# A hybrid decoder block on one core: gate tiles stored by chunk group, gathered rows spread over the dense loop, an 8-rank look-up and reciprocal roots on GpSimd

## The chip, the cores and the metric

The kernel runs on one core of a Trainium2 chip. A core has TensorE (PE in the profile, its weight loads PEld), VectorE (DVE), ScalarE (ACT), GpSimd (POOL) and SyncE (SP, which here only issues DMAs), a scratch memory of 128 partitions (SBUF), accumulators (PSUM) and 16 DMA engines to the DRAM. The metric is the time of one execution on the device in microseconds, the median of the runs.

## The reference

One decoder layer for 1024 tokens of width 1024, in float32:

```python
h  = rmsnorm(x, mix_norm)
zc = h @ w_in                                   # q|k|v, z, beta, alpha of the DeltaNet; q, k, v of the attention
o  = concat(gated_deltanet(...), swa_sink_attention(...))
x  = x + o @ w_out
x  = x + peer(rmsnorm(x, ffn_norm), peer_wq, peer_keys, peer_u, peer_v)
x  = x + sigmoid(rmsnorm(x, ple_norm) @ ple_gate) * (p @ ple_proj)
out = rmsnorm(x, final_norm)

def peer(h, wq, sub_keys, u_tab, v_tab):        # 8 heads, 128 x 128 experts, 16 per head and token
    qry = (h @ wq).reshape(T, 8, 2, 128)
    sc = einsum("thpd,hpnd->thpn", qry, sub_keys)
    top_s, top_i = top_k(sc, 16)
    cand_s = top_s[:, :, 0, :, None] + top_s[:, :, 1, None, :]
    best_s, best_pos = top_k(cand_s, 16)        # of the 16 x 16 sums
    expert = take(cand_i, best_pos);  gates = softmax(best_s)
    act = gelu(einsum("td,thkd->thk", h, u_tab[expert]))
    return einsum("thk,thkd->td", gates * act, v_tab[expert])
```

u_tab and v_tab have 16,384 rows of 1024 each.

## The kernel before

The tokens stand in 8 blocks of 128. Every matrix product with float32r operands splits both sides into a high and a low part and makes three products (`mm3`).

The program has three stages. **Upstream** (`upstream`): `project` multiplies x by w_in for the two halves of the tokens; then, for groups of two blocks, `mixers` (DeltaNet and attention) and `retrieve` (w_out, the norm, the queries, the first top-k, `topk`). `topk` finds the 16 best sums of each head and looks up which pair of ranks each one was: in steps of `KC` ranks it compares positions with constants and sums over 16 candidates by a tree of additions on `get3`.

**The two ways of PEER.** For the blocks in `ABLK` (5, 6, 7) the rows of u and v that each token chose are gathered by indirect DMA on GpSimd's queue: 128 fetches of u rows per block, each followed by a reduction on VectorE into `dots` (line 839), and 128 of v rows, each followed by an addition into `acc` (line 847). For the blocks in `BBLK` (0 to 4, `NT` = 640 tokens) everything is multiplied instead: `topk` builds a gate matrix of 128 x 128 experts per token. Four tokens at a time, VectorE makes two one-hot tiles (`o1`, `o2`), ScalarE scales `o2` by the gates, TensorE multiplies them into `bk_gm`, and ScalarE writes the result into `stage` (expert chunk by token). Every `TB` = 32 tokens a stage goes to `gd` in DRAM.

**The dense loop** (`dense`) runs over 128 chunks of 128 experts, in 32 groups of `GC` = 4. At a group's start the gate tile `Gt` is loaded (one buffer). Per chunk, u and v are loaded (`ur`, `vr`) and split, `bk_u` = u h is made in two parts of 320 tokens (24 matmuls each), ScalarE applies the gelu (`ge`), VectorE multiplies by `Gt` and splits the result into `wh` and `wl`. After four chunks, ten tiles of the output (5 blocks x 2 halves) are multiplied: four stay in PSUM (`bk_yp`) over all groups, six (`bk_y`, two banks) are added to `xB` on VectorE in every group. The gathering is a generator; after each chunk it is moved on by 6 rows, so that 24 rows per group are issued in the program's text ahead of the output tiles. Rows of block 5 use the 4 buffers of pool `gp`, those of blocks 6 and 7 also the 4 of `gx`.

**The last stage** (`final`) does the gate product, the projection and the final norm, block by block.

`rsqrt` makes a reciprocal root on VectorE by an integer guess and three Newton steps: 12 instructions. It is used for the 8 norms ahead of each of four products and twice per block in the DeltaNet, 48 times.

A scheduler places the instructions: it follows the order of the text as priority and a timeline of its own, and it fixes each engine's order when the program is built. On the chip each engine then runs its list in order. Where a tile's buffer is taken again, a wait stands in the queue that writes it.

Of the kernel before, what the change touches and what calls it, by code (L numbers as in the profile page):

```python
# [18 lines left out]
P = 128  # L19
# [8 lines left out]
GROUPS = [[0, 1], [2, 3], [4, 5], [6, 7]]  # L28
ABLK = [5, 6, 7]
BBLK = [0, 1, 2, 3, 4]  # L30
NA = len(ABLK)
GC = 4
TB = 32
GBUF = 4
GXBUF = 4
# [27 lines left out]
def block_kernel(ctx: ExitStack, tc, I, out, dbg=None):  # L63
    nc = tc.nc
    V, S, G, PE = nc.vector, nc.scalar, nc.gpsimd, nc.tensor
    NB = NBLK - NA
    NT = NB * P

# [39 lines left out]
    iota = cp.tile([P, P], F32, name="iota")  # L108
    sel_b = cp.tile([P, 3, 16, 8], BF, name="sel_b")
    early = ExitStack()  # L110
# [5 lines left out]
    UI, SL, ones = (C[n] for n in ("ui", "sl", "ones"))  # L116
# [3 lines left out]
    def load_consts():  # L120
        nc.sync.dma_start(ident, I["consts"][:, 0:P])
        nc.sync.dma_start(cst, I["consts"][:, P:])
        nc.sync.dma_start(iota, I["consts"][:, 4 * P:5 * P])
        V.tensor_copy(sel_b.rearrange("p s a h -> p (s a) h"), bc(sel[:, 58:106], 2, 8))
        V.memset(negt, NEG)
# [13 lines left out]
    h2d = dr.tile([max(NA, 1), P, D], F32, name="h2d")  # L139
    h2Td = [dr.tile([P, DK, NT], F32, name=f"h2Td{i}") for i in range(2)]  # L140
    gd = dr.tile([NT // TB, P, NE, TB], F32, name="gd")

    eidx = cp.tile([P, max(NA, 1), P], I32, name="eidx")
    gate_a = cp.tile([P, max(NA, 1), P], F32, name="gate_a")

    def rsqrt(pool, dst, src, scale, n):
        v = pool.tile([P, n], F32, tag=f"rsv{n}", name="rs_v")
        i = pool.tile([P, n], I32, tag=f"rsi{n}", name="rs_i")
        t = pool.tile([P, n], F32, tag=f"rst{n}", name="rs_t")
        V.tensor_scalar(v, src, scale, EPS, op0=ALU.mult, op1=ALU.add)  # L150
        V.tensor_scalar(i, v.bitcast(I32), 1, None, op0=ALU.logical_shift_right)
        V.tensor_scalar(i, i, -1.0, 1597463007.0, op0=ALU.mult, op1=ALU.add)
        y = i.bitcast(F32)
        for it in range(3):
            tt(t, y, y, ALU.mult)
            stt(t, t, -0.5, v, ALU.mult, ALU.mult)
            stt(dst if it == 2 else y, t, 1.5, y, ALU.add, ALU.mult)
# [169 lines left out]
    def upstream():  # L327
        with early as em:
            dn = em.enter_context(tc.tile_pool(name="dn", bufs=1, reuse_waits="tile"))
            psum(em, dn=2, de=1, sw=1)  # L330
            with ExitStack() as es:
# [21 lines left out]
                project(1, (c1, wp, sm))  # L353
            with ExitStack() as es:
                lt = es.enter_context(tc.tile_pool(name="lt", bufs=1, side="right", reuse_waits="tile"))
                retrieve = retrieving(lt, es)
                for gi in range(len(GROUPS)):
                    if gi + 1 < len(GROUPS):
                        mixers(gi + 1)
                    retrieve(gi)  # L360
# [20 lines left out]
    def retrieving(lt, es):  # L381
# [14 lines left out]
        def retrieve(gi):  # L396
# [9 lines left out]
            for ti in range(4):  # L406
# [11 lines left out]
                for bi in range(nb):  # L418
                    tt(xts[bi][:, cs], pcs[bi], xts[bi][:, cs], ALU.add)
            h2 = hp.tile([P, 2, DK, N], F32R, tag="h2", name="h2")  # L420
            h2h, h2l = h2[:, 0], h2[:, 1]
            for bi, b in enumerate(grp):
# [4 lines left out]
                if b in ABLK:  # L427
                    nc.sync.dma_start(h2d[ABLK.index(b)], h)
                transpose_split("s3", h, h2h, h2l, bs_)
                if b in BBLK:  # L430
                    t0 = (b - BBLK[0]) * P
# [4 lines left out]
            for q4 in range(4):  # L436
# [12 lines left out]
                for bi in range(nb):  # L449
# [5 lines left out]
                    for i in range(4):  # L455
                        first_topk(lt, sc[:, i], tv[bi][:, 4 * q4 + i], tiu[bi][:, 4 * q4 + i])
            for bi, b in enumerate(grp):
                topk(lt, bg, b, tv[bi], tiu[bi])

        return retrieve  # L460
# [52 lines left out]
    def deltanet(dn, dn_state, b, qkv_d, zc_d, g, beta, eg, mTh, mTl, cols):  # L513
# [3 lines left out]
        qkv = dn.tile([P, 12, P], F32, tag="qkv", name="qkv", bufs=2)  # L517
# [68 lines left out]
        for l in range(1, 7):  # L586
# [20 lines left out]
            if l < 6:  # L607
# [4 lines left out]
                copy(X, px)  # L612
        kb = scaled("kb", 4, cf[:, 2])
# [39 lines left out]
    def swa(dn, state, b, zc_d, cos, sin, sink, mTh, mTl, cols):  # L653
# [72 lines left out]
        state["kv"] = (kz, vz)  # L726

# [10 lines left out]
    def topk(tk, bg, b, v, iu):  # L738
# [13 lines left out]
        for h in range(8):  # L752
# [5 lines left out]
            V.max_index(out=pu[:, h, 8:16], in_max=bs[:, h, 8:16], in_values=c)  # L758
        pos = tk.tile([P, 16, 8], BF, tag="pos", name="pos")
# [6 lines left out]
        KC = 4  # L766
# [6 lines left out]
        for k0 in range(0, 16, KC):  # L773
# [13 lines left out]
            summed(i2.rearrange("p (h k) -> p k h", h=8)[:, ks], t3)  # L787

        ga = gate_a[:, ABLK.index(b)] if b in ABLK else bg.tile([P, P], F32, tag="ga", name="ga")
# [6 lines left out]
        tt(gv, gv, bc(gs, 2, 16), ALU.mult)  # L796
        if b in ABLK:
            stt(eidx[:, ABLK.index(b)], i1, 128.0, i2, ALU.mult, ALU.add)
            return
        pt = bank("gm", [4, P])  # L800
        tr(pt[:, 0], i1)
        tr(pt[:, 1], i2)
        tr(pt[:, 2], ga)
        tT = bg.tile([P, 3, P], F32, tag="tT", name="tT")
        copy(tT, pt[:, 0:3])
        NTK = 4
        for tb in range(P // TB):
            stage = bg.tile([P, NE, TB], F32, tag="stage", name="stage", bufs=2)
            for t8 in range(TB // NTK):
                c0 = tb * TB + t8 * NTK  # L810
                o1 = bg.tile([P, NTK, P], F32, tag="o1", name="o1", bufs=2)
                o2 = bg.tile([P, NTK, P], F32, tag="o2", name="o2", bufs=2)
                tt(o1, bc(iota, 1, NTK), bc(tT[:, 0, c0:c0 + NTK], 2, P), ALU.is_equal)
                tt(o2, bc(iota, 1, NTK), bc(tT[:, 1, c0:c0 + NTK], 2, P), ALU.is_equal)
                for i in range(NTK):
                    copy(o2[:, i], o2[:, i], scale=tT[:, 2, c0 + i:c0 + i + 1])
                for q in range(NTK // 4):
                    pg = bank("gm", [4, P])
                    for i in range(4):
                        mm(pg[:, i], o2[:, 4 * q + i], o1[:, 4 * q + i])  # L820
                    t0 = t8 * NTK + 4 * q
                    copy(stage[:, :, t0:t0 + 4].rearrange("p e t -> p t e"), pg)
# [225 lines left out]
```

## Time and profile before

| | |
|---|---|
| time, median of 3 runs | 3178.52 us (3174.45 to 3181.41) |
| span of the profiled execution | 3163.2 us, first to last instruction; its own time was not listed apart |
| TensorE busy | 2984.4 us (94%) |
| VectorE busy | 2601.3 us (82%) |
| ScalarE busy | 1296.5 us (41%) |
| GpSimd busy | 1028.0 us (32%) |
| moved by DMA | 869.38 MB, 275 GB/s on average |

In the profile's rows, a group of instructions shows its line, engine, operation, what it writes and reads, its count, then the busy time and the mean duration in ns, then the idle time of its engine just before it and what ended that. A matmul counts as busy until its modelled end. `L73`, `L76`, `L70` and `L128` are the lines of small helpers (`tt`, `stt`, `copy`, `mm`), so the tile names tell the place. A wait row reads: who waited, for whom, the sum in us, how often, the longest.

### The profile page before, as it was taken

What the parts mean: (1) busy time and instruction counts of PE and PEld (TensorE: products, weight loads), DVE (VectorE), ACT (ScalarE), POOL (GpSimd) and SP (SyncE); (2) the same over time, 40 slices, a digit from 0 to 9 for tenths busy, and PEclk for the clock granted to TensorE, in tenths of its full rate; (3) what the DMA queues carried; (4) which work ended last, traced back from release to release, by engine and by line L of the source; (5) the groups of instructions that cost most, each with busy time, mean ns of one, the idle gap of its engine ahead of it and who ended that gap; (6) DMA issues with size and microseconds to landing.
All of it is one profiled execution on the core that took longest, in us unless ns stands there. A gap on an engine that the chain in (4) does not pass through costs nothing. (4 is left out here: it accounts for less than half of the span.)

```text
span 3163.2 us, 50802 instructions
## 1 busy us (share of the span) xinstructions
PE 2984.4 (94%) x18287; PEld 2704.4 (85%) x18287; DVE 2601.3 (82%) x6191; ACT 1296.5 (41%) x2761; POOL 1028.0 (32%) x804
## 2 busy tenths in 40 slices
PE   7989989999897889899999999999999999999998
PEld 5878989899897878778888887988899889898887
DVE  6668636999899899789888887988988878799876
ACT  5577534488887862123222222222222122222232
POOL 0000000000000014445455565555565645566600
PEclk9999999999999999999999999999999999999999
DMA  7569566667578678778889888998998888999932
GB/s 232 159 240 353 171 213 225 207 228 248 199 242 321 235 274 283 279 263 298 292 297 316 305 310 310 338 353 304 340 334 309 315 317 321 327 328 345 334 140 87
DMA packets 366188, 869.38 MB, mean 275 GB/s; under 512 B 29296, under 2 KB 153584, under 8 KB 363120
## 3 DMA queue, kind: packets, MB, share of 16 engines
q1 hardware_dynamic: 255344, 463.43, 43.1%
q0 software_dynamic: 110592, 402.70, 35.3%
q8 instruction: 144, 2.36, 0.3%
q14 instruction: 108, 0.88, 0.1%
HBM read 766.40 MB, written 99.61 MB: 274 GB/s over the span
## 5 line engine op out<-in xcount | busy, mean ns | idle before, releaser
L128 PE MATMUL bk_u<-hT,uh 128*128 128x320 f32 x4096 | 919.4, 311 | 16.1 <-ACT ge L904 16.1
L833 POOL DMA_INDIRECT rows<-in_u_dram,eidx x384 | 495.1, 1289 | 893.6 <-DVE tiu L732 469.1
L128 PEld LDWEIGHTS bk_u<-hT,uh 128*128 128x128 f32 x4096 | 698.2, 189 | 36.6 <-ACT ge L904 19.3
L833 POOL DMA_INDIRECT rows<-in_v_dram,eidx x384 | 523.5, 1363 | 401.9 <-DVE acc L76 283.5
L128 PE MATMUL bk_u<-hT,ul 128*128 128x320 f32 x2048 | 635.8, 311 | 0.2 <-DVE ul L73 0.2
L76 DVE SCALAR_TENSOR_TENSOR acc<-rows,dots,acc 128x1024 f32<-128x1024 f32 x384 | 492.0, 1281 | 44.5 <-DMA rows<-in_v_dram,eidx 41.3
L839 DVE CUSTOM_DVE_ANT_0 rows<-rows,h2n 128x1024 f32<-128x1024 f32 x384 | 461.8, 1221 | 37.3 <-DMA rows<-in_u_dram,eidx 31.5
L128 PEld LDWEIGHTS bk_u<-hT,ul 128*128 128x128 f32 x2048 | 387.5, 189 | 5.0 <-DVE ul L73 0.5
L904 ACT ACTIVATE ge<-bk_u 128x320 f32<-128x320 f32 x256 | 110.3, 432 | 642.1 <-PE bk_u L128 541.9
L128 PE MATMUL bk_y<-vh,wh 128*128 128x512 f32 x768 | 313.1, 408 | 40.2 <-DVE xB L73 38.2
L70 ACT ACTIVATE wh<-ge 128x320 fp32r<-128x320 f32 x256 | 119.0, 470 | 525.6 <-DVE ge L73 466.7
L128 PE MATMUL bk_y<-vl,wh 128*128 128x512 f32 x768 | 308.5, 402 | 0.0
L128 PE MATMUL bk_y<-vh,wl 128*128 128x512 f32 x768 | 304.3, 402 | 2.2 <-DVE wl L73 1.8
L128 PE MATMUL bk_gm<-o,o 128*128 128x128 f32 x1280 | 205.4, 292 | 29.6 <-ACT o L70 27.6
L70 ACT ACTIVATE o<-o,tT 128x128 f32<-128x128 f32 x640 | 202.4, 396 | 40.0 <-DVE o L73 34.7
L73 DVE TENSOR_TENSOR o<-iota,tT 128x512 f32<-128x512 f32 x320 | 205.4, 686 | 13.8 <-PE bk_gm L128 12.9
L128 PE MATMUL bk_yp<-vh,wh 128*128 128x512 f32 x512 | 202.3, 400 | 13.5 <-ACT wh L70 13.5
L128 PEld LDWEIGHTS bk_gm<-o,o 128*128 128x128 f32 x1280 | 182.2, 200 | 37.1 <-ACT o L70 33.9
L73 DVE TENSOR_TENSOR ge<-ge,Gt 128x320 f32<-128x320 f32 x256 | 123.7, 487 | 108.7 <-DMA Gt<-gd 95.2
L128 PEld LDWEIGHTS bk_y<-vh,wh 128*128 128x128 f32 x768 | 147.8, 192 | 76.2 <-DVE xB L73 43.2
L128 PE MATMUL bk_s<-h,whi 128*128 128x256 f32 x1024 | 206.8, 294 | 5.2 <-ACT h L70 1.5
L128 PE MATMUL bk_yp<-vl,wh 128*128 128x512 f32 x512 | 201.8, 398 | 0.0
(308 smaller groups left out, 6001.8 us busy)
## 6 DMA issues: line engine op xcount, KB each, us to landing
ur<-in_uT_dram SPq DMA_DIRECT2D x128, 512.0 KB
vr<-in_v_dram SPq DMA_DIRECT2D x128, 512.0 KB
gd<-stage SPq DMA_DIRECT2D x20, 2048.0 KB
Gt<-gd SPq DMA_DIRECT2D x32, 1280.0 KB
wlo<-wqc SPq DMA_DIRECT2D x128, 256.0 KB
whi<-wqc SPq DMA_DIRECT2D x128, 256.0 KB
whi<-woc SPq DMA_DIRECT2D x64, 256.0 KB
wlo<-woc SPq DMA_DIRECT2D x64, 256.0 KB
```

The source lines that it names most:

```text
L70: return S.activation(o, i, AF.Copy, **k)
L73: return V.tensor_tensor(o, a, b, op)
L76: return V.scalar_tensor_tensor(o, a, s, b, op0, op1, **k)
L128: PE.matmul(o, l, r, start=start, stop=stop)
L833: G.indirect_dma_start(out=r, out_offset=None, in_=tab, in_offset=bass.IndirectOffsetOnAxis(ap=eidx[:, a, s:s + 1], axis=0))
L839: V.tensor_tensor_reduce(out=u, in0=u, in1=h2n, op0=ALU.mult, op1=ALU.add, scale=1.0, scalar=0.0, accum_out=dots[:, s:s + 1])
L904: S.activation(ge, pa, AF.Gelu_apprx_tanh)
```

## The change

- **Gate tiles.** `gd` is laid out by chunk group, [32 groups, 128, 40, 4, 16], and `TB` is 16. A group's `Gt` is now one contiguous run of 10 KB in each partition; a store of a stage (1 MB, 40 of them) has 32 runs of 256 bytes in each partition. The stage is evicted with the token as the innermost index, in runs of 4.
- **Rows.** The generator is moved on after each chunk and after each output tile, 768 rows over 448 steps. Each row's VectorE instruction is given a dependency on the dense loop's VectorE instruction three steps back (`LAG` = 2), which only sets the order. All three blocks take even rows from `gp` (4 buffers, opened before the last groups of the upstream stage) and odd rows from `gx` (3).
- **Chunks.** The next chunk's u and v are loaded and split in the text ahead of the output tiles (`prepared`).
- **Look-up.** `KC` is 8 in place of 4.
- **Roots.** `rsqrt` becomes a multiply-add and a power of -0.5 on GpSimd.
- **Space.** `qkv` has one buffer in place of two, the gates of blocks 0 to 4 take a part of `cand`, `iota` is read from the constants' tile.

`HBLK` is empty, so the branches for it, and the calls of `tick` in the upstream stage (no job is set there), issue nothing.

```diff
-BBLK = [0, 1, 2, 3, 4]
+DBLK = [0, 1, 2, 3, 4]
 ABLK = [5, 6, 7]
+BBLK = HBLK + DBLK          # HBLK = []
 GC = 4
-TB = 32
+TB = 16
 GBUF = 4
-GXBUF = 4
+GXBUF = 3
+LAG = 2
...
-    gd = dr.tile([NT // TB, P, NE, TB], F32, name="gd")
+    gd = dr.tile([NE // GC, P, NT // TB, GC, TB], F32, name="gd")
...
     def rsqrt(pool, dst, src, scale, n):
-        v = pool.tile([P, n], F32, tag=f"rsv{n}", name="rs_v")
-        i = pool.tile([P, n], I32, tag=f"rsi{n}", name="rs_i")
-        t = pool.tile([P, n], F32, tag=f"rst{n}", name="rs_t")
-        V.tensor_scalar(v, src, scale, EPS, op0=ALU.mult, op1=ALU.add)
-        V.tensor_scalar(i, v.bitcast(I32), 1, None, op0=ALU.logical_shift_right)
-        V.tensor_scalar(i, i, -1.0, 1597463007.0, op0=ALU.mult, op1=ALU.add)
-        y = i.bitcast(F32)
-        for it in range(3):
-            tt(t, y, y, ALU.mult)
-            stt(t, t, -0.5, v, ALU.mult, ALU.mult)
-            stt(dst if it == 2 else y, t, 1.5, y, ALU.add, ALU.mult)
+        v = pool.tile([P, n], F32, tag=f"rsv{n}", name="rs_v", bufs=2)
+        G.tensor_scalar(v, src, scale, EPS, op0=ALU.mult, op1=ALU.add)
+        G.tensor_tensor(dst, v, mhalf[:, 0:n], ALU.pow)
...
-        KC = 4
+        KC = 8
...
+            for t0 in range(0, TB, 4):
...
-                    copy(stage[:, :, t0:t0 + 4].rearrange("p e t -> p t e"), pg)
-            nc.sync.dma_start(gd[(b - BBLK[0]) * (P // TB) + tb], stage)
+                copy(stage[:, :, t0:t0 + 4], pg.rearrange("p t e -> p e t"))
+                yield
+            nc.sync.dma_start(gd[:, :, BBLK.index(b) * (P // TB) + tb].rearrange("g p c t -> p g (c t)"),
+                              stage.rearrange("p (g c) t -> p g (c t)", c=GC))
...
+    def fetched(gp, tab, u, s):
+        r = (pools["gx"] if "gx" in pools and s % 2 else gp).tile([P, D], F32, tag="rows", name="rows")
...
+            held_back(stt(acc, v, w[:, s:s + 1], acc, ALU.mult, ALU.add))
...
+    def held_back(ins):
+        if len(anchors) > LAG:
+            tc.add_manual_dep(ins.ins, anchors[-1 - LAG].name, ...)
...
+            def step(ins):
+                anchors.append(ins.ins)
+                count[0] += 1
+                n = total * count[0] // steps - count[1]     # steps = NE + NE // GC * NB * 2
+                count[1] += n
+                advance(n)
...
-                nc.sync.dma_start(Gt.rearrange("p t g k -> p t (g k)"),
-                                  gd[:, :, cg * GC:(cg + 1) * GC, :].rearrange("t p g k -> p t (g k)"))
+                nc.sync.dma_start(Gt, gd[cg])
...
-                    want = total * (c + 1) // NE
-                    while done < want and next(job, "end") != "end":
-                        done += 1
+                    if c + 1 < NE:
+                        nxt = prepared(c + 1)
+                    step(last)
...
                         if not keep or cg == NE // GC - 1:
-                            tt(xB[:, bi, cs], py, xB[:, bi, cs], ALU.add)
+                            last = tt(xB[:, bi, cs], py, xB[:, bi, cs], ALU.add)
+                        step(last)
```

Three places show what the scheduler makes of it. The first is SP's queue while the gates of block 2 go out; `whi` and `wlo` are the weights that TensorE needs for the queries of the next group, `keysT` the keys. Before:

```order
L393 DMA wlo_12244<-wqc1_85 128x512
L439 DMA keysT_12202<-in_keysT_dram 128x512
L823 DMA gd_72<-stage_9550 128x4096
L392 DMA whi_12274<-wqc0_84 128x512
L393 DMA wlo_12275<-wqc1_85 128x512
L392 DMA whi_12278<-wqc0_84 128x512
L393 DMA wlo_12279<-wqc1_85 128x512
```

And after the change:

```order
L394 DMA wlo_11959<-wqc1_86 128x512
L849 DMA gd_73<-stage_9332 128x32x64
L441 DMA keysT_11917<-in_keysT_dram 128x512
L393 DMA whi_11989<-wqc0_85 128x512
L849 DMA gd_73<-stage_9390 128x32x64
L394 DMA wlo_11990<-wqc1_86 128x512
L393 DMA whi_11993<-wqc0_85 128x512
L394 DMA wlo_11994<-wqc1_86 128x512
```

Stores stand twice as often among the weight loads, each of half the bytes, and each waits in this queue for its stage.

The second place is VectorE's list in the middle of the dense loop, where the output tiles of one group are added to `xB` while v rows are gathered. Before:

```order
L76 SCALAR_TENSOR_TENSOR acc_22999<-rows_23185,dots_20180,acc_22999 128x1024
L73 TENSOR_TENSOR xB_14844<-bk_y_23343,xB_14844 128x512
L76 SCALAR_TENSOR_TENSOR acc_22999<-rows_23188,dots_20180,acc_22999 128x1024
L76 SCALAR_TENSOR_TENSOR acc_22999<-rows_23191,dots_20180,acc_22999 128x1024
L73 TENSOR_TENSOR xB_14844<-bk_y_23357,xB_14844 128x512
L76 SCALAR_TENSOR_TENSOR acc_22999<-rows_23194,dots_20180,acc_22999 128x1024
L76 SCALAR_TENSOR_TENSOR acc_22999<-rows_23197,dots_20180,acc_22999 128x1024
L76 SCALAR_TENSOR_TENSOR acc_22999<-rows_23200,dots_20180,acc_22999 128x1024
L73 TENSOR_TENSOR xB_14844<-bk_y_23371,xB_14844 128x512
```

And after the change:

```order
L82 SCALAR_TENSOR_TENSOR acc_22342<-rows_23152,dots_19673,acc_22342 128x1024
L79 TENSOR_TENSOR xB_14178<-bk_y_23155,xB_14178 128x512
L82 SCALAR_TENSOR_TENSOR acc_22342<-rows_23169,dots_19673,acc_22342 128x1024
L82 SCALAR_TENSOR_TENSOR acc_22342<-rows_23172,dots_19673,acc_22342 128x1024
L79 TENSOR_TENSOR xB_14178<-bk_y_23175,xB_14178 128x512
L82 SCALAR_TENSOR_TENSOR acc_22342<-rows_23189,dots_19673,acc_22342 128x1024
L82 SCALAR_TENSOR_TENSOR acc_22342<-rows_23192,dots_19673,acc_22342 128x1024
L79 TENSOR_TENSOR xB_14178<-bk_y_23195,xB_14178 128x512
```

In the steady loop two or three rows stand between two additions to `xB` both before and after; the count no longer swings by three.

The third place is VectorE's list at the end of the dense loop and the start of the last stage, where `rs_t` and `rs_i` belong to a root, `h` to a norm, `wgl` to the gate weights. Before:

```order
L73 TENSOR_TENSOR rs_t_31092<-rs_i_31091 128x1
L76 SCALAR_TENSOR_TENSOR rs_t_31092<-rs_t_31092,rs_v_31090 128x1
L76 SCALAR_TENSOR_TENSOR rs_31089<-rs_t_31092,rs_i_31091 128x1
L73 TENSOR_TENSOR xB_14844<-bk_y_30899,xB_14844 128x512
L76 SCALAR_TENSOR_TENSOR h_31086<-xt_31082,rs_31089,ple_norm_30990 128x1024
L73 TENSOR_TENSOR xB_14844<-bk_y_30913,xB_14844 128x512
L73 TENSOR_TENSOR xB_14844<-bk_y_30927,xB_14844 128x512
L73 TENSOR_TENSOR xB_14844<-bk_y_30941,xB_14844 128x512
L73 TENSOR_TENSOR xB_14844<-bk_y_30955,xB_14844 128x512
```

And after the change:

```order
L79 TENSOR_TENSOR xB_14178<-bk_y_30260,xB_14178 128x512
L82 SCALAR_TENSOR_TENSOR acc_27716<-rows_30274,dots_25127,acc_27716 128x1024
L79 TENSOR_TENSOR xB_14178<-bk_y_30280,xB_14178 128x512
L82 SCALAR_TENSOR_TENSOR acc_27716<-rows_30277,dots_25127,acc_27716 128x1024
L82 SCALAR_TENSOR_TENSOR acc_27716<-rows_30294,dots_25127,acc_27716 128x1024
L82 SCALAR_TENSOR_TENSOR acc_27716<-rows_30297,dots_25127,acc_27716 128x1024
L82 SCALAR_TENSOR_TENSOR h_30326<-xt_30322,rs_30329,ple_norm_30320 128x1024
L79 TENSOR_TENSOR wgl0_30351<-raw_30352,wgh0_30350 128x1024
```

The last rows now stand behind the last output tile, and the first norm of the last stage behind them; the steps of the roots are gone from this list.

More of the change, by code (lines that the diff above doesn't have):

```diff
@@ L827, in gather_block, with gather_dots @@
+    def gather_dots(gp, u):
         h2n = gp.tile([P, D], F32, tag="hacc", name="h2n", bufs=1)
-        nc.sync.dma_start(h2n, h2d[a])
+        nc.sync.dma_start(h2n, h2d[u])
         dots = gp.tile([P, P], F32, tag="dots", name="dots", bufs=1)
-        def rows(tab, s):
-            r = (gx if a and s % 2 else gp).tile([P, D], F32, tag="rows", name="rows")
-            G.indirect_dma_start(out=r, out_offset=None, in_=tab,
-                                 in_offset=bass.IndirectOffsetOnAxis(ap=eidx[:, a, s:s + 1], axis=0))
-            return r
@@ L847, in gather_block, with half_job, gather_job, advance @@
         for s in range(P):
-            v = rows(I["v"], s)
-            stt(acc, v, w[:, s:s + 1], acc, ALU.mult, ALU.add)
+            v = fetched(gp, I["v"], u, s)
+            held_back(stt(acc, v, w[:, s:s + 1], acc, ALU.mult, ALU.add))
             yield
         nc.sync.dma_start(x1d[b], acc)
-    def gather_job(gp):
-        for a in range(NA):
-            yield from gather_block(gp, a)
+    def half_job():
+        for b in HBLK:
+            w = yield from gather_dots(pools["gp"], UBLK.index(b))
+            pt = bank("gm", [P])
+            tr(pt, w)
+            copy(slots[b][:, 2], pt)
+    anchors = []
+    def held_back(ins):
+        if len(anchors) > LAG:
+            tc.add_manual_dep(ins.ins, anchors[-1 - LAG].name,
+                              mybir.DependencyInfo(mybir.DependencyClass.NoSync, mybir.DependencyReason.DATA),
+                              reason="gather behind dense")
+    pools = {}
+    credit = [0.0]
+    def gather_job():
+        for b in ABLK:
+            yield from gather_block(pools["gp"], b)
+    def advance(n):
+        job = pools.get("job")
+        while job is not None and n > 0:
+            if next(job, "end") == "end":
+                pools["job"] = job = None
+            n -= 1
+    def drain():
+        advance(1 << 20)
+    def tick(us):
+        credit[0] += us * RATE
+        n = int(credit[0])
+        credit[0] -= n
+        advance(n)
     def dense(xB):
         with ExitStack() as es:
-            gp = es.enter_context(tc.tile_pool(name="gp", bufs=GBUF, reuse_waits="tile"))
             pp = es.enter_context(tc.tile_pool(name="pp", bufs=1, reuse_waits="tile"))
@@ L867, in dense @@
             held = {(bi, j): bank("yp") for bi in range(HELD) for j in range(2)}
-            hT = [pp.tile([P, DK, NT], F32R, name=f"hT{i}") for i in range(2)]
+            hT = [pp.tile([P, DK, NU], F32R, name=f"hT{i}") for i in range(2)]
             for i in range(2):
```

166 lines of the change are left out of this document (104 added, 62 removed).

## The prediction

> **What bounds the kernel now.** I read the busy shares by stage first, with borders at three events of the rows: the end of the gate building, the first product with a gate tile, and the last product of the dense loop.
>
> ```profile
> core 0: us, PE busy (x) PEld busy (x) DVE busy (x) ACT busy (x) POOL busy (x), PEclk, DMA share, GB/s
> 625.00:1150.00 525.00, 480.88 (x3837) 463.96 (x3835) 494.35 (x2037) 434.96 (x1083) 1.03 (x4) 0.97 0.70 243
> 1167.60:1923.40 755.80, 706.08 (x3772) 626.94 (x3771) 628.50 (x1149) 183.42 (x298) 383.08 (x293) 0.97 0.85 295
> 1923.40:3052.00 1128.60, 1115.09 (x6144) 1002.83 (x6144) 962.00 (x1327) 289.79 (x475) 631.38 (x473) 0.99 0.90 321
> 3052.00:3163.20 111.20, 97.22 (x448) 78.99 (x446) 79.46 (x239) 40.99 (x68) 0.00 (x0) 0.95 0.26 90
> 700.00:800.00 100.00, 99.13 (x845) 96.98 (x845) 98.73 (x420) 86.58 (x220) 0.00 (x0) 1.00 0.70 240
> ```
>
> From 625 to 1150 us the gates of blocks 0 to 4 are built, and VectorE is the fullest engine: 494 of 525 us. TensorE reads 481, but its 3837 matmuls go at 845 in 100 us where nothing holds it (last row), so it needs about 454 us. After 1167.6 us comes the dense loop, 32 groups of four chunks. Its pace, where it runs free, is in the chain that ended last:
>
> ```profile
> 2287.57 5.60 PE bk_y L128 x24
> ...
> 2343.72 5.60 PE bk_y L128 x24
> ...
> 2399.86 5.60 PE bk_y L128 x24
> ```
>
> One group is 56.15 us of pure TensorE. The loop has 32 x 56.15 = 1797 us of it, less about 7 us of a first chunk that is multiplied before 1167.6, so 1790; it takes 1884. So 94 us are lost there, nearly all in the first 756 us, where twelve groups (674 us less those 7) lose about 89. The waits say to what:
>
> ```profile
> DVE ge L73 <- DMA Gt<-gd: 95.2, 19, 8.6
> PE bk_y L128 <- DVE xB L73: 38.2, 15, 6.7
> DVE rows L839 <- DMA rows<-in_u_dram,eidx: 23.1, 26, 3.5
> DVE acc L76 <- DMA rows<-in_v_dram,eidx: 41.3, 36, 5.8
> 1904.76 0.08 DVE L839 DVE_READ_ACCUMULATOR2_ANT dots<- 128x1 f32 x1
> 1913.41 0.89 DVE L73 TENSOR_TENSOR ge<-ge,Gt 128x320 f32<-128x320 f32 x2 [8.58 <-DMA Gt<-gd]
> 1344.93 0.80 PE L128 MATMUL bk_y<-vh,wh 128*128 128x512 f32 x1 [6.65 <-DVE xB L73]
> ```
>
> VectorE stands 95 us for the gate tile (one buffer; its load starts when the last product of the group before has read it), 23 us for gathered u rows (up to 1500 us) and 41 us for v rows (1500 to 1850 us), in order, so the additions to xB behind it come late and TensorE finds no free bank. The clock column drops to 0.97 there.
>
> **The change, part by part.**
>
> *Gate tiles by group.* The load of a gate tile becomes 128 runs of 10 KB instead of 2560 of 512 bytes. The store becomes 163,840 runs of 256 bytes (40 x 128 x 32) instead of 2560 of 16 KB. Prices of a packet:
>
> ```profile
> q1 hardware_dynamic: 255344, 463.43, 43.1%
> q0 software_dynamic: 110592, 402.70, 35.3%
> q1 hardware_dynamic: 528, 0.26, 39.6%
> q1 hardware_dynamic: 47903, 126.85, 69.0%
> ```
>
> (The third row is a stretch of 2.2 us with one store to DRAM in 512-byte runs, the fourth 625 to 1150.) Shares are of 16 engines over the span of 3163.2 us: q0 161.5 ns for 3641 bytes, q1 85.4 ns for 1815 bytes, on average. The line through both is 9.8 ns + 0.0417 ns a byte: 31 ns at 512 bytes (the store itself: 0.396 x 16 x 2200 / 528 = 26 ns), 692 at 16 KB, and 20.4 ns at 256 bytes, an estimate. Loads: a group's tile takes 160 packets x 31 ns = 5.0 us per engine, interleaved with rows; after it 8 x 437 ns = 3.5 us, in 8 turns instead of 160. The 95 us of waits should go. Stores: 163,840 x 20.4 / 16 = 209 us of all engines against 2560 x 692 / 16 = 111. That is +98 us in 625 to 1150, where they were 0.70 x 525 = 368 us busy: 466.
>
> The Trainium skill, page "DMA: Bandwidth & Descriptors", section Specifications, asks for "≥512 B (below this, SDMA does read-modify-write)". No store of before is that short, so no run shows it; the rival below has its price.
>
> *Eviction.* ScalarE writes the stage with a stride; after the change it writes runs of four and reads PSUM with a stride.
>
> ```profile
> L70 ACT ACTIVATE stage<-bk_gm 128x512 f32<-128x512 f32 x160 | 170.4, 1091 | 28.0 <-PE bk_gm L128 27.0
> L70 ACT ACTIVATE X<-bk_dn 128x512 f32<-128x512 f32 x40 | 23.9, 599 | 38.6 <-PE bk_dn L131 38.6
> L76 DVE SCALAR_TENSOR_TENSOR rs_t<-rs_t,rs_v 128x1 f32<-128x1 f32 (+2 forms) x144 | 22.4, 158 | 2.5
> L73 DVE TENSOR_TENSOR get<-get 128x256 bf16<-128x256 bf16 x96 | 27.2, 284 | 0.5
> L73 DVE TENSOR_TENSOR get<-get 128x128 bf16<-128x128 bf16 x96 | 21.4, 222 | 0.4
> L73 DVE TENSOR_TENSOR get<-get 128x64 bf16<-128x64 bf16 x96 | 17.7, 184 | 0.4
> L73 DVE TENSOR_TENSOR get<-pos,sel_b 128x512 bf16<-128x512 bf16 x32 | 13.3, 417 | 0.2
> ```
>
> Between 0.60 (contiguous) and 1.09 us each, I take 0.72: 160 x 0.37 = 59 us less on an engine that has 90 us free in that stretch. Worth nothing by itself; it keeps ScalarE from being the next bound.
>
> *Powers on GpSimd.* 48 reciprocal roots of 12 VectorE steps at 0.157 us become two GpSimd steps each. VectorE is rid of 576 x 0.157 = 90 us, 60 of it ahead of the dense loop, the rest in the last stage.
>
> *Look-up of eight ranks.* 160 steps of 512 at 0.418 become 80 of 1024 at about 0.67 (0.5 ns an element by the rows of 128 and 256): 67 to 54 us. The trees, 96 x (0.284 + 0.222 + 0.184) = 66 us, become 48 x (0.41 + 0.284 + 0.222) = 44. Minus 35 us on VectorE.
>
> *Upstream sum.* About 60 of these 95 us lie in 625 to 1150 (nearly all of the look-up, half of the roots): VectorE 434, which at its present share of 0.94 makes a stretch of 461 (-64). TensorE allows 454 (-71). The DMA engines, at 0.94 (the fullest group of the dense loop shows that share), allow 466 / 0.94 = 496: **-29**. Late next is the weight load behind the stores on SP's queue. I take the smallest. Ends: -71, and +87 from the rival.
>
> *GpSimd's own price.*
>
> ```profile
> L679 POOL COPY vz<-qk 128x64 f32<-128x64 f32 x16 | 4.4, 306 | 419.6 <-DMA qk<-zcn 419.6
> L833 POOL DMA_INDIRECT rows<-in_u_dram,eidx x384 | 495.1, 1289 | 893.6 <-DVE tiu L732 469.1 <-DVE dots L839 294.6 <-issue 53.0
> POOL vz L675 <- PE bk_sw L128: 187.5, 5, 70.9
> 1846.99 6.39 DMA x1d<-acc
> 1853.39 3.85 DMA h2n<-h2d
> ```
>
> No power is in the trace. Two steps cost 0.6 us at the copy's price, 2.6 at the row fetch's, for 1.9 on VectorE: -1.3 to +0.7 a root, for 32 roots ahead of the loop -42 to +22 if all were exposed. I take 0: other blocks' work covers them, and a step of that few elements is nearest to the copy. If the cover fails, it is because they queue in order behind the clearing of vz, which waited up to 71 us for TensorE. The halved buffer of qkv costs a load of 768 KB per block behind the same cover: 0 to 8 x 3 us.
>
> *Rows spread and held.* No work is added; the order behind dense steps costs no semaphore, being on one engine. The first block gets seven buffers instead of four (later ones seven instead of eight), which removes most of the 64 us of row waits. What stays: the order puts 31 rows and the rest of the look-up into the first two groups, 126 us of VectorE at the rows' durations against 112 of TensorE, 14 us; and at five turns between u and v rows, and between blocks, VectorE waits for a store and a load (10 us, rows above) and catches up with 4.5 us of slack per group: 4 us each, 20. So 34 of 94 stay: **-60**, ends -85 and -15.
>
> *End.* Three row additions stand behind the last xB, 3 x 1.28 = 3.8 us, before the gate weights are split; the last root saves 1.3: **+2**.
>
> **Sum.** -29 - 60 + 2 = -87. The profiled execution spans 3163.2 us, 15 below the median of the runs shown, 3178.5, which I take as the frame around it: 3178.5 - 87 = 3091.5.
>
> **Rivals.**
>
> 1. *Short stores (slower).* If a 256-byte store costs no less than one of 512 (31 ns), the stores take 318 us, the DMA engines need 575, the stretch is 575 / 0.94 = 612, +87, and the time is 3178.5 + 87 - 60 + 2 = 3207. The sign turns at 28.4 ns a packet. For it: no shorter store is in the trace. Against it: the line through the two queues has a start of only 9.8 ns. If a short store is read and written back, two passes of 31 ns each, it is 637 us, a stretch of 951 and a time near 3547. The page named above says so; by its rule alone the change would be far slower.
> 2. *The dense loop keeps its loss.* VectorE works about 51 of 56 us in a group whatever feeds it; a row that lands late (the longest wait was 5.8 us) then stalls TensorE as the gate tile did. If 80 of the 94 us stay: 3178.5 - 29 - 14 + 2 = 3137. For it: one buffer fewer later on. Against: groups with eight buffers ran at 56 us.
> 3. *The engines allow more.* If the stores hide and VectorE sets the pace (-64), and only 19 us stay in the loop (-75): 3041.
> 4. *It does nothing*: the stores take back what the loop gains, by chance within 6 us of the old time.
>
> **How the numbers follow.** Forecast 0.59 (3050 to 3125 as its own range), rival 1 0.13, rival 2 0.14, rival 3 0.11, rival 4 0.03. Change within 0.2% (6 us, about what a measurement of this kernel can tell) is "same": 0.03; slower is rival 1, 0.13; faster the rest, 0.84. The range runs from 3035, just past rival 3, to 3165, which takes in rival 2 and a dearer GpSimd; rival 1 and a little at the bottom are left out.
>
> **What would show it.** Right: dense groups of 56 us from the first, hardly a wait of ge for Gt; the gate building shorter by some 30 us, with the DMA share there near 0.9; evictions near 0.7 us; VectorE's total down by about 125 us. Wrong: 256-byte packets well over 20 ns, or TensorE waiting for whi and wlo; GpSimd roots of several us, or stuck behind vz; waits of acc for rows in the later groups.

## The result, and the profile after

The changed kernel takes **3061.69 us** (median of 4 runs, 3061.11 to 3063.47), the kernel before 3178.68 (4 runs, 3174.45 to 3181.41): a ratio of 0.964, 95% interval 0.9623 to 0.9656, so 3.6% or 117 us less. Forecast were 3091.5 us and 87 less. One of the ten runs of roots_dve, below, took 5912 us; its ratio is without that run, its median is over all ten (3162.6 over the other nine).

The windows of the changed kernel, with borders at the same events as the prediction's (end of the gate building, first product with a gate tile, and, added here, the first such product of the third group, then the last matmul of the loop), and below them those of the kernel before for the same pieces. The columns are those of the prediction's first table: busy time and count of PE, PEld, DVE, ACT and POOL, then granted clock, DMA share and GB/s.

```profile
0.00:614.80 614.80, 581.14 (x4080) 529.83 (x4081) 391.47 (x1051) 333.45 (x798) 36.59 (x77) 0.98 0.69 231
614.80:1114.20 499.40, 462.26 (x3717) 447.08 (x3717) 473.93 (x1768) 376.58 (x1111) 22.63 (x30) 0.97 0.85 244
1149.60:1269.90 120.30, 101.78 (x546) 90.31 (x545) 112.57 (x308) 34.15 (x53) 41.77 (x33) 0.91 0.69 245
1269.90:2949.10 1679.20, 1674.90 (x9347) 1521.61 (x9345) 1463.38 (x1990) 438.63 (x719) 974.49 (x731) 1.00 0.91 329
```

```profile
0.00:644.50 644.50, 594.60 (x4182) 540.22 (x4183) 438.93 (x1446) 352.61 (x880) 8.60 (x33) 0.98 0.68 226
644.50:1150.80 506.30, 465.69 (x3723) 449.67 (x3721) 476.97 (x1951) 422.77 (x1033) 0.72 (x3) 0.97 0.69 244
1167.60:1278.60 111.00, 100.99 (x563) 91.04 (x561) 91.92 (x250) 29.29 (x47) 46.64 (x39) 0.98 0.84 295
1278.60:3052.00 1773.40, 1720.18 (x9352) 1538.72 (x9353) 1498.58 (x2225) 443.92 (x726) 967.82 (x726) 0.98 0.88 311
```

From the third group to the last matmul: 1773.4 us before, 1679.2 now, in which TensorE is busy 1674.9, at a granted clock of 1.00 (0.98 before). That is 94 of the 101.5 us between the two profiled executions. Up to the third group there is little: 1278.6 against 1269.9. The gates are finished 36.6 us earlier (1150.8 to 1114.2), the first product comes 18 us earlier (1167.6 to 1149.6), and after two groups 9 us are left of it. VectorE's waits now and one of TensorE's, over the whole span (who waited, for whom, sum, times, longest):

```profile
DVE rows L864 <- DMA rows<-in_u_dram,eidx: 42.4, 38, 2.8
DVE acc L82 <- DMA rows<-in_v_dram,eidx: 7.0, 8, 1.9
...
PE bk_y L134 <- DVE xB L79: 17.0, 4, 14.4
```

The 95 us for Gt are not in the list any more, the v rows' 41 are 7, and TensorE's 38 us for xB are 17, of which 14.4 are one wait, in the second group. The waits for u rows have not become shorter (42.4 against 31.5), but they cost TensorE little: 37.0 of the 42.4 lie behind the third group's start, where TensorE is idle for 4.3 us in all.

### The profile page after: what moved, and what is told of

Read it like the earlier page. It is cut to its first block, busy times and chain, and to the rows that moved or that the text cites. A ratio compares the mean times of both kernels' runs of the same rounds, so it can differ in the third digit from the quotient of the medians.

```text
span 3061.7 us, 50184 instructions
## 1 busy us (share of the span) xinstructions
PE 2943.6 (96%) x18287; PEld 2694.2 (88%) x18287; DVE 2527.3 (83%) x5327; ACT 1232.8 (40%) x2761; POOL 1092.6 (36%) x901
## 5 line engine op out<-in xcount | busy, mean ns | idle before, releaser
L854 POOL DMA_INDIRECT rows<-in_u_dram,eidx x384 | 516.7, 1346 | 539.6 <-DVE dots L864 328.4
L854 POOL DMA_INDIRECT rows<-in_v_dram,eidx x384 | 504.0, 1312 | 374.2 <-DVE acc L82 301.1
L864 DVE CUSTOM_DVE_ANT_0 rows<-rows,h2n 128x1024 f32<-128x1024 f32 x384 | 457.0, 1219 | 50.1 <-DMA rows<-in_u_dram,eidx 42.4
L134 PE MATMUL bk_y<-vh,wh 128*128 128x512 f32 x768 | 301.6, 393 | 17.7 <-DVE xB L79 17.0
L79 DVE TENSOR_TENSOR o<-cst,tT 128x512 f32<-128x512 f32 x320 | 204.7, 682 | 10.9 <-PE bk_gm L134 9.0
L76 ACT ACTIVATE vh<-vr 128x1024 fp32r<-128x1024 f32 x128 | 132.0, 1054 | 181.7 <-PE bk_y L134 100.5
L76 ACT ACTIVATE uh<-ur 128x1024 fp32r<-128x1024 f32 x128 | 135.3, 1057 | 160.4 <-PE bk_u L134 143.4
```

Source lines behind the costliest of these rows:

```text
L76: return S.activation(o, i, AF.Copy, **k)
L79: return V.tensor_tensor(o, a, b, op)
L134: PE.matmul(o, l, r, start=start, stop=stop)
L854: G.indirect_dma_start(out=r, out_offset=None, in_=tab, in_offset=bass.IndirectOffsetOnAxis(ap=eidx[:, u, s:s + 1], axis=0))
L864: held_back(V.tensor_tensor_reduce(out=r, in0=r, in1=h2n, op0=ALU.mult, op1=ALU.add, scale=1.0, scalar=0.0, accum_out=dots[:, s:s + 1]))
```

## The experiments

Each kernel was run beside the one before the change; ratios are to that. A variant is planned afresh by the scheduler, which moves instructions far from the edit too, so I read stages rather than totals where the two part. A table first, from the traces: when the last gates were evicted, when VectorE started the last expert indices of block 7 (`eidx`, the end of the look-up), when it started the first addition to xB, when the first product with the third group's gate tile came, and how long it was from there to the end of the last matmul (us).

| kernel | gates done | last eidx | first xB | third group | rest of the loop |
|---|---|---|---|---|---|
| before | 1151 | 1651 | 1219 | 1279 | 1773 |
| gate_only | 1135 | 1646 | 1234 | 1287 | 1741 |
| roots_only | 1152 | 1647 | 1223 | 1284 | 1771 |
| changed | 1114 | 1220 | 1221 | 1270 | 1679 |
| old_gate | 1164 | 1246 | 1258 | 1320 | 1699 |
| rows_chunk | 1118 | 1289 | 1289 | 1335 | 1708 |
| no_hold | 1117 | 1286 | 1286 | 1331 | 1706 |
| four_bufs | 1115 | 1223 | 1223 | 1270 | 1723 |
| roots_dve | 1134 | 1306 | 1306 | 1356 | 1682 |
| kc4 | 1123 | 1228 | 1228 | 1279 | 1686 |
| gate_rows | 1145 | 1286 | 1287 | 1341 | 1677 |
| tree_pool | 1136 | 1283 | 1283 | 1338 | 1676 |
| late_rows | 1115 | 1203 | 1216 | 1262 | 1672 |
| late_split | 1116 | 1206 | 1216 | 1257 | 1678 |

### The gate tiles

**gate_only**: the kernel before with the new layout, `TB` and eviction.

```diff
-    gd = dr.tile([NT // TB, P, NE, TB], F32, name="gd")
+    gd = dr.tile([NE // GC, P, NT // TB, GC, TB], F32, name="gd")
...
-                    copy(stage[:, :, t0:t0 + 4].rearrange("p e t -> p t e"), pg)
+                    copy(stage[:, :, t0:t0 + 4], pg.rearrange("p t e -> p e t"))
...
+                nc.sync.dma_start(Gt, gd[cg])
```

> The kernel before with the gate part of the change alone: gate tiles stored by chunk group (TB 16, runs of 256 bytes), evicted in runs of 4 tokens, loaded as 10 KB runs. Rows, look-up and roots as before. Theory A (each part pays for its own wait): the 95 us of ge waiting for Gt go almost whole, the dense loop goes from 1884 to about 1835, and the gate building gains 0 to 10 us; about 3120 us. Rival B (the gate tile's wait only stands in front of the row waits, as in the prediction's second rival): waits of VectorE for rows grow by about what the Gt waits lose, dense loop above 1870, about 3165 us. Rival C (short stores cost): gate building above 520 us, SP's queue late with weights.

Measured: 3137.31 us, ratio 0.9872 (0.9838 to 0.9907). Its row waits and VectorE's wait for TensorE's output tiles, with no row of ge for Gt left, and below them that last wait in the kernel before:

```profile
DVE rows L840 <- DMA rows<-in_u_dram,eidx: 44.7, 35, 4.4
DVE acc L76 <- DMA rows<-in_v_dram,eidx: 41.4, 27, 5.9
DVE xB L73 <- PE bk_y L128: 98.8, 66, 5.5
```

```profile
DVE xB L73 <- PE bk_y L128: 59.7, 43, 3.8
```

All 95 us of Gt waits went, but the loop became only 27 us shorter (1884 to 1857). VectorE's waits for u rows grew from 31.5 to 44.7 us, those for v rows stayed at 41, and the largest growth is in the wait for `bk_y`, 39 us: part of the time that VectorE stood for the gate tile it would otherwise have stood for TensorE. So the truth lies between A and B. C fell: the gate building was 489 us long, shorter than before's 506.

**old_gate**: the changed kernel with the old layout, `TB` 32 and one stage buffer.

> The changed kernel with the gate tiles back in the old layout (TB 32, stores of 16 KB runs, strided eviction, loads in 512-byte runs). The stage has one buffer, since two of that size do not fit beside the gather buffers, so the gate building is slower for a reason of its own and only the dense loop, from the first product with a gate tile to the last matmul, is read against the changed kernel's 1799.5 us. Theory A: in the late groups the load of 22 us hides behind TensorE's own 20 us from the last product of a group to the first of the next; in the crowded first twelve it does not: ge waits for Gt 30 to 60 us in all, dense loop 1820 to 1850. Rival B (spread rows leave VectorE enough slack, the layout is worth nothing by then): below 1808. Rival C (the layout carries all of the gain): above 1860.

Measured: 3125.43 us, ratio 0.9826 (0.9795 to 0.9857); 546 us of gate building (499 in the changed kernel), as the one buffer would have it. From its first product the loop took 1829.5 us, 30 more than the changed kernel's 1799.1; Gt waits were 34.9 us in 6 waits. Theory A holds. Both ways the layout is worth about 30 us in the loop, a third of the 95 us that VectorE waited for Gt in the kernel before.

### The rows

**rows_chunk**: rows issued after chunks alone, nothing held back; seven buffers kept. The line taken out is the one behind each output tile.

```diff
-            steps = NE + NE // GC * NB * 2
+            steps = NE
...
-                        step(last)
...
-        if len(anchors) > LAG:
+        if len(anchors) > 1 << 20:
```

> The changed kernel with the rows issued as before: 6 rows in the program's text after each chunk, none after the output tiles, and no dependency that holds them back. The seven buffers for all blocks, the early load of the next chunk and the new gate layout stay. Theory A (spreading and holding are what lets VectorE keep up in the first groups): TensorE waits again for xB and wl, dense loop 1799.5 to 1820-1835, about 3085 to 3095 us. Rival B (the buffers and the gate layout do it, the spreading only looks tidy): within 6 us of 3062.

Measured: 3159.25 us, ratio 0.9947 (0.9925 to 0.9968). Both theories were wrong in size: it is 98 us slower than the changed kernel, most of what the whole change brought. The second group took 134.8 us instead of 82.2.

**no_hold**: only the last line of that diff.

> The changed kernel without the dependency that holds rows back; the spreading over 448 steps stays. Issuing rows after chunks alone and without it cost 97 us, 65 of them in the first three groups, where 64 rows went ahead of block 7's look-up and that look-up ahead of xB, and 29 in the later groups. Theory A (the dependency does the first part, the spreading the second): third group 40 to 65 us later, later groups within 8 us of 1679, 3105 to 3130. Rival B (spreading does both): within 8 us of 3062. Rival C (the dependency does both): 3145 to 3160.

Measured: 3153.95 us, ratio 0.9932 (0.991 to 0.9953). Rival C: the dependency does both, and the even spreading without it nothing that shows (3159 and 3154). Of the 92 us, 61 lie ahead of the third group's start and 27 in the groups after it. Holding rows back without spreading them was not run. TensorE's waits of the two, and VectorE's list in no_hold where the long wait ends:

```profile
PE bk_y L134 <- DVE xB L79: 86.1, 12, 72.3
```

```profile
PE bk_y L134 <- DVE xB L79: 80.2, 9, 70.0
```

```profile
1285.47 0.27 DVE L79 TENSOR_TENSOR cand<-get 128x64 f32<-128x64 bf16 x1
1285.77 0.29 DVE L82 SCALAR_TENSOR_TENSOR eidx<-cand 128x128 int32<-128x128 f32 x1
1285.98 1.28 DVE L79 TENSOR_TENSOR xB<-bk_y,xB 128x512 f32<-128x512 f32 x2
```

The first addition to xB stands right behind the last step of block 7's look-up. Without the dependency VectorE does 64 rows ahead of that point, among the steps of the left-over look-up (9 in the changed kernel), and TensorE stands for 70 us. The same lines of the changed kernel:

```profile
1220.13 0.27 DVE L79 TENSOR_TENSOR cand<-get 128x64 f32<-128x64 bf16 x1
1220.43 0.29 DVE L82 SCALAR_TENSOR_TENSOR eidx<-cand 128x128 int32<-128x128 f32 x1
1220.64 1.28 DVE L79 TENSOR_TENSOR xB<-bk_y,xB 128x512 f32<-128x512 f32 x2
```

**four_bufs**: rows of block 5 from four buffers again.

```diff
-        r = (pools["gx"] if "gx" in pools and s % 2 else gp).tile(...)
+        r = (pools["gx"] if "gx" in pools and u and s % 2 else gp).tile(...)
```

> The changed kernel in which the rows of block 5 use the four buffers of the first pool alone, as before the change; those of blocks 6 and 7 keep seven. Theory A (the seven buffers took away most of the 64 us of row waits): with four, a fetch of some 7 us to landing against a row every 2.3 us leaves 2 us of spare, VectorE waits for rows of block 5 again, TensorE behind it, and the first eleven groups take 15 to 40 us more, 3077 to 3102. Rival B (even spreading does what the buffers would): within 6 us of 3062.

Measured: 3100.5 us, ratio 0.9752 (0.9728 to 0.9776), 39 us slower than the changed kernel; in the traces all of it lies behind the third group's start (1270 in both; 1723 against 1679 after it). VectorE's waits of this kernel between 1270 and 1930 us, and below them the changed kernel's there:

```profile
DVE acc L82 <- DMA rows<-in_v_dram,eidx: 38.4, 31, 4.1
DVE rows L864 <- DMA rows<-in_u_dram,eidx: 36.0, 31, 4.5
```

```profile
DVE rows L864 <- DMA rows<-in_u_dram,eidx: 10.8, 8, 2.2
DVE acc L82 <- DMA rows<-in_v_dram,eidx: 3.5, 3, 1.9
```

74 us of waits against 14: theory A, at the top of its range.

### VectorE's relief

**roots_dve**: the changed kernel with the 12 steps of `rsqrt` on VectorE. **roots_only**: the kernel before with the two steps on GpSimd. The edit is the `rsqrt` piece of the diff above, backward and forward.

> The changed kernel with the reciprocal roots back on VectorE (12 steps each). VectorE gets back the 66 us that the roots took there as a union of their spans. Theory A (the upstream stage is paced by VectorE, 95% busy while the gates are built): 20 to 35 us slower, nearly all before the end of the gate building (1114 us), about 3090. Rival B (the roots lie beside other work, the look-up gave the gain): within 6 us of 3062. Rival C (GpSimd's in-order queue makes its roots late): faster than 3056.

> The kernel before with the roots alone moved to GpSimd. Putting them back on VectorE cost the changed kernel 101.6 us, though their union there is 66 us. Theory A (VectorE's upstream work in front of the dense loop is a queue: what doesn't fit ends up in the first groups, ahead of the additions to xB, so that relief pays one for one or more, but only where the rows don't already stand in the way): before the change the rows and the gate tile hold the first twelve groups anyway, so the relief shows upstream alone, gate building over 15 to 25 us earlier, 3150 to 3165 us. Rival B (the roots are worth the same everywhere): 3075 to 3100. Rival C (their place in the order decides, not their time): within 6 us of 3177, or slower.

Measured: roots_dve 3163.32 us, ratio 0.9961 (0.9947 to 0.9976), 102 us slower than the changed kernel; roots_only 3160.57 us, ratio 0.994 (0.9921 to 0.9958). The same relief is worth about 19 us in the one and 102 in the other. In roots_dve the gates are done 20 us later, and 64 of the 102 us lie in the first two groups. Of these, 51 lie in the first group, which took 88.7 us instead of 38.1, and there TensorE is hardly idle: it still has queries (`bk_s`) and keys of the last blocks to multiply, until 1221 us, where the changed kernel had done them by 1133. The other 13 lie in the second group, where the last look-up ends at 1306 and TensorE waits for xB. The queries' products in roots_dve between 1172 and 1222 us, and the wait for xB behind them:

```profile
L134 PE MATMUL bk_s<-h,whi 128*128 128x256 f32 x160 | 29.2, 283 | 0.0
```

```profile
PE bk_y L134 <- DVE xB L79: 31.3, 3, 29.8
```

All three expectations for the first kernel fell. For the second, the time lies in theory A's range, but not by its mechanism: the gates were to be done 15 to 25 us earlier, and they are done at 1152 us (1151 before). Its gate building starts 7.5 us earlier (637.0 against 644.5) and takes 9 us more. The traced run of roots_only is as long as that of the kernel before (spans of 3163.6 and 3163.2 us), so these two traces do not show where the 19 us lie.

**kc4**: `KC = 4` again. **gate_rows**: that and the roots on VectorE.

> The changed kernel with the look-up in steps of 4 ranks. VectorE gets back 20 us as a union of spans (109 against 89 in the traces). Theory A (capacity ahead of the loop): about 20 us more, half of it before the end of the gate building and half as a longer wait of TensorE for xB in the second group; 3075 to 3095. Rival B (any other order of VectorE's list upsets the first groups, however little work it adds): 3110 or more. Rival C (hidden): within 6 us of 3062.

> The changed kernel with the roots back on VectorE and the look-up in steps of 4, so the gate layout and the rows' part of the change without the relief of VectorE. In every variant of the changed kernel so far the first addition to xB came at the moment when the last expert indices of block 7 (eidx) were written; in the kernel before, that look-up was spread among the rows until 1651 us. Theory A (holding the rows back lets the whole left-over look-up go ahead of xB; that pays only if the relief makes it short): the third group starts at about 1356 + 10 = 1366 us, 85 us later than before the change, the groups after it run at 56 us, and the whole is 3165 to 3185, no faster than before, and 30 to 45 us slower than the gate part alone (3137). Rival B (the parts add up: roots and look-up gave 30 us upstream, as the prediction's first term has it): about 3062 + 30 = 3090.

Measured: kc4 3078.78 us, ratio 0.9695 (0.9669 to 0.9721), 17 us slower than the changed kernel, as A has it; the gates are done 8 us later, but only 4 us more are lost in the first two groups, and 7 in the later ones. gate_rows 3132.28 us, ratio 0.9844 (0.9814 to 0.9874). Its theory A is right in kind (third group late, at 1341; rest of the loop 1677) and wrong in size: it has more work on VectorE than roots_dve and is 31 us faster. Its last look-up is done at 1286 instead of 1306, and TensorE's last product with the keys is at 1185 instead of 1221, ahead of the first group and not in it. So it makes tens of us where the scheduler places the last queries and the last top-k; no variant changes that place alone. The roots cost between 53 us (gate_rows less kc4) and 102, by what else is in the kernel. Without the relief, the rows' part brings nothing that can be told from the gate part alone (0.9844 against 0.9872, with overlapping intervals).

**tree_pool**: the additions of the look-up's trees on GpSimd.

```diff
-                tt(x[:, 0:16:2 * s], x[:, 0:16:2 * s], x[:, s:16:2 * s], ALU.add)
-            tt(dst, x[:, 0], x[:, 8], ALU.add)
+                G.tensor_tensor(x[:, 0:16:2 * s], x[:, 0:16:2 * s], x[:, s:16:2 * s], ALU.add)
+            G.tensor_tensor(dst, x[:, 0], x[:, 8], ALU.add)
```

> The changed kernel with the additions of the look-up's trees on GpSimd: 192 steps, some 58 us on VectorE as the rows have them. Theory A (VectorE paces the gate building at 95% and what is left over stalls the loop's start): the gate building falls from 499 towards TensorE's 454 to 470 us and the leftover shrinks, 20 to 45 us faster, 3017 to 3042. Rival B (GpSimd's queue runs in order, stands for up to 99 us behind a root that waits, and a float step there is several times dearer; the look-up then is late and the rows with it): slower than 3080. Rival C (a step on GpSimd slows VectorE beside it, so that nothing is won): within 6 us of 3062.

Measured: 3123.53 us, ratio 0.9828 (0.98 to 0.9856), 62 us slower than the changed kernel. Groups of this kernel, with the idle time of GpSimd ahead of them:

```profile
L785 POOL TENSOR_TENSOR get<-get 128x512 bf16<-128x512 bf16 x48 | 63.3, 1320 | 277.5 <-DVE get L79 267.6 <-DVE gs L811 9.9
L785 POOL TENSOR_TENSOR get<-get 128x256 bf16<-128x256 bf16 x48 | 40.2, 837 | 3.7
```

Rival B: a step of 512 elements takes 1.32 us (0.41 on VectorE in the changed kernel), the queue stands for 268 us for VectorE's products, the gate building grows to 525 us and the last look-up ends at 1283.

### The start of the loop

**late_rows**: no rows in the first 21 of 448 steps. **late_split**: that, and `vl` of the first seven chunks on GpSimd (the last line).

```diff
-                n = total * count[0] // steps - count[1]
+                n = max(0, total * (count[0] - 21) // (steps - 21)) - count[1]
...
+                split(vr, vh, vl, G if c < 7 else V)
```

> The changed kernel with no rows issued during the first 21 of its 448 steps (one and a half groups); the 768 rows are spread over the other 427. VectorE has 50 us of upstream work left when the loop begins, and TensorE waits 14.4 us for xB in the second group. Theory A (the leftover and the early rows together are more than VectorE can do there, 126 against 112 us): that wait shrinks or goes, 5 to 15 us faster, 3047 to 3057. Rival B (the wait is set by the order alone, the leftover stands ahead of xB with or without rows): within 6 us of 3062. Rival C (the later groups, with 25.2 rows instead of 24, lose it again): slower than 3066.

> The changed kernel with no rows in the first 21 of 448 steps (that alone: 3057.9, TensorE's wait for xB 8.4 us) and the low parts of v for the first seven chunks made on GpSimd, seven steps of 1.22 us less on VectorE before the first addition to xB. Theory A (the leftover ahead of xB is what TensorE waits for): the wait falls by 5 to 8 us and the kernel to 3048 to 3053. Rival B (a step of that size on GpSimd takes 2.5 us or more by the tree's steps, 1.3 us for 512 two-byte elements, and TensorE waits for vl instead): 3058 or more.

Measured: 3057.85 us, ratio 0.963 (0.9606 to 0.9654), and 3056.49 us, ratio 0.9614 (0.9594 to 0.9634). Neither interval stands apart from the changed kernel's 0.9623 to 0.9656. In late_rows the look-up ends at 1203, but TensorE still waits 8.4 us for xB, and VectorE 12.3 for its load (SP's timeline, then VectorE's):

```profile
1202.17 0.43 SPq L933 DMA_DIRECT2D xB<-x1d  x1
```

```profile
1215.86 1.29 DVE L79 TENSOR_TENSOR xB<-bk_y,xB 128x512 f32<-128x512 f32 x2 [12.27 <-DMA xB<-x1d]
```

The 2560 KB of xB are issued at 1202 us; between the first gate tile's load and this one SP's queue has eleven loads of u and v and the second gate tile. Before the change it was at 1145. In the changed kernel it is issued at 1202.27 and takes 10.7 us to land, so 1213 is the earliest first addition there, and the look-up's 1220 hides it. In late_split the wait for xB is gone (the third group starts 12 us earlier than in the changed kernel), and the end takes 120.9 us instead of 112.6, where TensorE waits 13.1 us for block 7's norm (5.8 in the changed kernel), which needs the last rows; late_rows has the same at its end (119.5 and 13.0). An xB load ahead of the u and v loads was not tried.

## Why the prediction was right, and where it was not

**Sum.** Against the profiled executions, as the prediction made it:

| term | predicted | measured |
|---|---|---|
| up to the first product with a gate tile | -29 | -18.0 |
| dense loop | -60 | -84.9 |
| end | +2 | +1.4 |
| span | -87 | -101.5 |
| time over span | 15.3 kept | 1.8 |

The time lies 30 us below the forecast: upstream gave 11 us less than taken, the loop 25 more, and 15 come from the frame.

**The frame, mis-sized by 13.5 us.** The prediction took the 15.3 us between span and median as a fixed surround. The changed kernel's profiled run took 3063.47 us with a span of 3061.7: 1.8 us around it, and 1.7 to 2.1 in every run of the experiments. With those 1.8 the profiled execution of the kernel before took 3165.0, less than any of its timed runs (3168 to 3187 in all series): a quick one of a kernel that spreads over some 17 us in a series, where the changed kernel's runs spread over 2.4.

**Upstream: near in size for the gates by luck, wrong in the step.** They are finished 36.6 us earlier (-29 taken). But the gate building itself, for which the 29 were worked out, shrank by 6.9 us only, and 29.7 came ahead of it, where the sum has no term. The relief of VectorE shows there: with the roots back the gate building starts at 628.9 us, with the 4-rank look-up at 626.9, with both at 649.2, against 614.8 in the changed kernel and 644.5 before. The bound named for the gate building, the DMA engines at 466 us of work, was not reached: the share of 0.85 is 424 us, and VectorE is still the fullest engine with 474 of 499 us. Two sizes failed. A short store is cheaper than the line said; the stretch of 2.5 us with nothing but 256-byte stores in the changed kernel:

```profile
DMA packets 2281, 0.58 MB, mean 234 GB/s; under 512 B 2281, under 2 KB 2281, under 8 KB 2281
...
q1 hardware_dynamic: 2281, 0.58, 92.1%
```

0.921 x 16 x 2500 / 2281 = 16.2 ns a packet, not 20.4, and about half of the 31 taken for 512 bytes. Rival 1 is out, and so is what hung on the Trainium skill, page "DMA: Bandwidth & Descriptors", section Specifications: if a store under 512 bytes was read and written back here, it did not show as the two passes of the rival. And VectorE's relief is less than counted: its busy time fell by 74 us (2601.3 to 2527.3), not 125. Steps of one engine overlap at their ends in the traces. The 576 root steps add up to 90 us, but only 66 of them lie behind the end of the step before; so counted, the steps that write `get` fell from 102 to 85 us, and not by 34 as their durations did (133 to 99).

**What gave half of it back.** 18.6 of the 36.6 us are lost between the last gate and the first product with one. The prediction costed the stores, not the load that waits for the last of them on SP's queue, before and after:

```profile
SPq L880 <- DMA gd<-stage: 7.7, 1, 7.7
```

```profile
SPq L965 <- DMA gd<-stage: 19.4, 1, 19.4
```

That is 11.7 of the 18.6 us. Two loads of `hT`, 2560 KB each, are issued just ahead of that store (at 1116 and 1117 us; before the change at 998), and it takes 20.0 us to land, where the median store takes 7 to 8. The rest is 3 us until the store is issued and 4 us more from the gate tile's issue to its first use.

**Dense loop: 94 us lost before, 34 foreseen.** In the first two groups TensorE waits 14.4 us for xB; 14 were said for them. At the turns less stays than 20: from the third group on TensorE idles for 4.3 us (1679.2 - 1674.9). And 15 us come from a quantity that I held fixed, the pace of a free group. In the changed kernel the first `bk_y` of two groups in a row:

```profile
2147.52 0.39 PE L134 MATMUL bk_y<-vh,wh 128*128 128x512 f32 x1
2203.18 0.39 PE L134 MATMUL bk_y<-vh,wh 128*128 128x512 f32 x1
```

That is 55.66 us where it was 56.15; times 32 it is some 15 us. Without that the loop's gain is about 69 for 60. The 15 us are worth that only in a loop that runs free: in roots_only a free group takes 55.65 us as well, and from the third group on it is 2 to 3 us shorter than before. Rivals 2 and 4 are out; the time lies between the forecast and rival 3.

**The separable terms were the weakest assumption.** Upstream and loop were costed apart. Taken out one at a time, the gate layout is worth 64 us (30 of it in the loop, the rest with the stage's one buffer), holding the rows 92, the buffers 39, eight ranks 17, the roots 102: 314 us for a change of 117. They are not separate: with roots and look-up both taken back the kernel loses 71 us, less than with the roots alone. Most of what holding (53 us) and the roots (64) cost lies at one place, the first two groups; the buffers' 39 lie behind it. In every variant with the change's loop, held or not, the first xB follows the last eidx within 13 us, in most at once: VectorE does the whole left-over look-up of blocks 6 and 7 ahead of the first addition to xB, and the later groups are free of it (in the kernel before, it lay among the rows until 1651 us). Holding keeps the rows out of that look-up, and the relief makes it short. What in the new loop brings the look-up ahead of xB is not shown; the early load of the next chunk (`prepared`), the earlier opening of `gp` and the single buffer of `qkv` were not taken out.

**GpSimd, eviction.** A root of one element per partition takes 0.40 + 0.68 us there, in the range of 0.3 to 1.3 a step (the power of eight elements takes 1.70), and no wait of VectorE for a root exceeds 2.4 us in the changed kernel:

```profile
L155 POOL TENSOR_TENSOR rs<-rs_v,mhalf 128x1 f32<-128x1 f32 x32 | 21.7, 678 | 2.7
...
L154 POOL TENSOR_SCALAR rs_v<-ss 128x1 f32<-128x1 f32 x32 | 12.8, 399 | 452.1 <-ACT h L188 421.8 <-DVE cand L79 27.0 <-DVE xB L79 3.3
...
L76 ACT ACTIVATE stage<-bk_gm 128x512 f32<-128x512 f32 x160 | 93.1, 587 | 44.5 <-PE bk_gm L134 40.8 <-DMA gd<-stage 3.3
```

The eviction takes 0.587 us, as little as the contiguous copy of the same size in the kernel before (0.599), not 0.72. That it is worth nothing by itself was not run.

## What to carry to other kernels

Where two stages overlap, ask which of the leftovers of the first stands ahead of the first result that the second needs in the same engine's list: here the same relief upstream was worth 19 us in one order and 53 to 102 in others. A wait that the profile summed to 95 us was worth 30: without it the same engine waited longer for others, and the buffers and the order had to come with it. And before a span is scaled to a median, look at what lies around the span in a run that has both.

## Not expected of the hardware

- The spacing of the 128x512 products of the loop, where TensorE was not held up, was 233.5 to 233.6 ns on average in two kernels (before, gate_only) and 229.0 to 229.2 in the twelve others, at a granted clock of 0.99 to 1.00 in both kinds. Common to those twelve is a constant of 32 bytes per partition (`mhalf`), allocated ahead of the other tiles; roots_only differs from the kernel before in little else. Whether the shifted addresses do it was not tried.
- A 256-byte store took 16.2 ns, with 234 GB/s in that stretch.
- GpSimd's float step of 512 two-byte elements took 3.2 times VectorE's (1.32 against 0.41 us), one of 128 elements 2.8 times (0.613 against 0.216).
